# A hybrid encoder step: one table of durations for making and ranking the work, another for ordering each engine's instructions

## The chip, the cores and the metric

The kernel runs on one core of a Trainium2 chip. The core has a matrix engine (TensorE, PE in the profile, with its weight loads shown as PEld), a vector engine (VectorE, DVE), a scalar engine (ScalarE, ACT), a general one (GpSimd, POOL), and a queue that issues most DMAs (SyncE, SP). Each works through its own list of instructions in order, and they meet through semaphores. The metric is the time of one execution on the device in microseconds.

## The reference, cut to what matters

Two layers for a prompt of 2048 tokens and a running stream of 32 further ones, of width 1024, in float32. The first layer is sliding-window attention with ALiBi and sinks, the second a gated DeltaNet; both have a normalization ahead, a SiLU gate and a residual add.

```python
def attn_prompt(h, w_in, sinks, w_out):
    q, k, v, gate = attn_project(h, w_in)
    ...
    o = sink_attention(qb, band(k), band(v), q_pos, k_pos.astype(F32), k_pos >= 0, sinks)
    y = (o * jax.nn.silu(gate)) @ w_out

def gated_delta_chunked(q, k, v, g, beta, s0, chunk):
    ...
    a = m + jnp.eye(chunk, dtype=F32)
    sol = lax.linalg.triangular_solve(a, rhs, left_side=True, lower=True, unit_diagonal=True)
    ...
    def step(s, xs):
        qi, ki, ui, wi, gi, ai = xs
        v_new = ui - jnp.einsum('bhcd,bhde->bhce', wi, s)
        o = jnp.einsum('bhcd,bhde->bhce', qi * jnp.exp(gi)[..., None], s) + jnp.einsum('bhij,bhje->bhie', ai, v_new)
        s = s * jnp.exp(g_last)[..., None, None] + jnp.einsum(
            'bhcd,bhce->bhde', ki * jnp.exp(g_last[..., None] - gi)[..., None], v_new)
        return s, o
```

The large matrix products (both layers' input and output projections) and the many small ones (scores, values, the chain over chunks of 64 tokens) all run on TensorE.

## The kernel before

**How the work is cut.** The prompt's tokens are four slabs of 512 columns (`SLABS`, line 30); the second also carries the 32 sample tokens, and so is cut in two groups of 272. For every slab, a block (class `Block`) is one projection of 128 output rows: eight 128-row steps of the inner dimension, three matmuls each, because every operand is split into a high and a low part of the fast float32 type (`project`). These are the matmuls `pj<-hk,wh` of the profile. Each block's result is taken from one of two banks `pj` by ACT or DVE.

**Sides.** Whatever isn't a projection is written as generators, called sides, which the builder advances between the matmuls of the blocks (`spawn`, `step`). In the attention layer a side (`attend`) computes two scores banks (`ta`), adds the bias and takes the maximum on DVE (`s<-ta,bias`, `mx`), takes the exponential on ACT (`s<-s,mx`), normalizes on DVE (`s<-s,den`), transposes on PE (`tb<-con,s`), copies on ACT (`pt`) and multiplies by the values (`tc<-pt,vt`). In the delta layer, `local_quad` makes the local scores, `inverse` solves the triangular systems on DVE (31 rounds of a product `sub` and a subtraction `tl`, with 32x32 transposes `ml`, `tq`, `trc` around), and `chain_quad` is the chain over chunks: PE `tb<-st,kq`, DVE `r`, PE `tb<-r,btt`, ACT `vn`, PE `tc<-vn,kd`, `tb<-vn,kd` and `tb<-vn,bit`, DVE `st`. Convolution and gates (`conv_block`, `z_block`) run on ACT, DVE and POOL from tiles `cx` and `cy`.

**The first estimate.** Nothing is sent to the engines while the sides run. Every call goes through `Engine.__getattr__` (line 176), which asks `Estimate.note` for a cost and hands an `Op` to `Order.add`. `Estimate` keeps a clock for each engine from two tables, `COST` (a fixed part, one per element, and one for a scalar that is taken from a tile; line 91) and `LAG` (from the end of an instruction on one engine to the start of the next on another; line 82). That clock says when a side may take its next step, hence where in the program its instructions are made, when weight halves are split, and from which matmul on a DMA may be issued. An instruction's rank is its place in this program, less a lead for a few (`EVAC` 400 for taking a bank, `CHAIN` 600 for the chain).

**The order of each engine.** `Order.flush`, called once at the end of each layer, plays all instructions through once more. It keeps a time for each engine; an instruction is ready when what it depends on has ended, plus the lag (`settle`); the engine that is free first takes the lowest rank among its ready instructions, and its clock advances by the instruction's cost. The sequence in which they are taken is the sequence in which each engine has them on the chip. In the kernel before, `flush` uses the costs of `Estimate.note` and its `LAG`. DMAs are played through too: 60 ns on the queue's engine, 1.5 us to start, a transfer time from size, and 0.5 us to land.

Of the kernel before, what the change touches and what calls it, by code (L numbers as in the profile page):

```python
# [12 lines left out]
F32R = mybir.dt.float32r  # L13
AF = mybir.ActivationFunctionType
ALU = mybir.AluOpType
# [7 lines left out]
CH = 64  # L23
# [33 lines left out]
class Block:  # L57
# [3 lines left out]
    def __init__(self, src, run, need=None, ahead=None, pre=None, post=None, ks=range(KT)):  # L61
        self.beside = False
        self.src, self.run, self.need, self.ahead, self.pre, self.post, self.ks = src, run, need, ahead, pre, post, ks
# [13 lines left out]
class Estimate:  # L77
# [4 lines left out]
    LAG = {  # L82
        "tensor": {"tensor": 0, "vector": 200, "scalar": 200, "gpsimd": 200},
        "vector": {"tensor": 256, "vector": 127, "scalar": 130, "gpsimd": 155},
        "scalar": {"tensor": 270, "vector": 145, "scalar": 34, "gpsimd": 160},
        "gpsimd": {"tensor": 200, "vector": 60, "scalar": 75, "gpsimd": 100},
    }
    MEAN = 200
# [11 lines left out]
    def place(self, pool, tag, bufs, name):  # L100
        ring = self.ring.setdefault((id(pool), tag), [])
        self.write[name] = (self.over(pool, tag, bufs), "")
        ring.append(name)
# [67 lines left out]
class Engine:  # L171
# [5 lines left out]
    def __getattr__(self, op):  # L177
        call = getattr(self.engine, op)

        def made(*args, **kw):  # L180
            is_ap = lambda x: isinstance(x, bass.AP)
            outs = [x for x in ([] if "out" in kw else [args[0]]) + [kw.get("out"), kw.get("accum_out")] if is_ap(x)]
            ins = [x for x in list(args[0 if "out" in kw else 1 :]) + [v for k, v in kw.items() if k not in ("out", "accum_out")] if is_ap(x)]
            cost = self.est.note(self.name, op, outs, ins, kw)
            self.order.add(Op(self.name, lambda: call(*args, **kw), cost, op == "dma_start"), ins, outs)  # L185

        return made

# [7 lines left out]
class Op:  # L196


    def __init__(self, engine, call=None, cost=0.0, dma=False):
        self.engine, self.call, self.cost, self.dma = engine, call, cost, dma  # L200
        self.after, self.left, self.ends, self.done, self.rank = [], 0, {}, False, 0
        self.gang = None


class Place:
# [6 lines left out]
class Order:  # L212
# [15 lines left out]
    @contextmanager  # L228
    def together(self):

        self.gang = Op(None)
        self.ops.append(self.gang)
        yield
        self.gang = None

    def place(self, pool, tag, bufs, name):
        ring = self.rings.setdefault((id(pool), tag), [])
# [57 lines left out]
    def settle(self, op):  # L295

        if op.engine:
            lag = lambda by: self.est.LAG.get(by, {}).get(op.engine, self.est.MEAN)
            heapq.heappush(self.wait[op.engine], (max([end + lag(by) for by, end in op.ends.items()] + [0.0]), op.rank, op))
        else:  # L300
            self.finish(op)
# [11 lines left out]
    def flush(self):  # L313

        overs = []
        for p in self.places.values():
            if p.old and p.over is None:
                p.over = Op(None)
                overs.append(p.over)
                for o in p.old.ops:  # L320
                    self.link(o, p.over)
                for o in {id(o): o for o in p.ops}.values():
                    self.link(p.over, o)
                    if o.gang:
                        self.link(p.over, o.gang)
        self.wait = {e: [] for e in self.ENGINES}
        ready = {e: [] for e in self.ENGINES}
        for o in [o for o in overs + self.ops if o.left == 0]:
            self.settle(o)
        while any(self.wait.values()) or any(ready.values()):  # L330
            when = {e: max(self.free[e], 0.0 if ready[e] else self.wait[e][0][0]) for e in self.ENGINES if ready[e] or self.wait[e]}
            e = min(when, key=when.get)
            now = when[e]
            while self.wait[e] and self.wait[e][0][0] <= now:
                _, rank, o = heapq.heappop(self.wait[e])
                heapq.heappush(ready[e], (rank, o))
            _, op = heapq.heappop(ready[e])
            op.call()
            if op.dma:
                self.free[e] = now + 60  # L340
                self.dma = max(now + 1500, self.dma) + op.cost * (self.CLOSE if now < self.START else 1)
                op.ends = {"dma": self.dma + 500}
            else:
                self.free[e] = now + op.cost
                op.ends = {e: self.free[e]}
            op.start = now
            self.finish(op)
        assert all(o.done for o in self.ops)
        self.ops = []
# [1903 lines left out]
```

## Time and profile before

| what | value |
|---|---|
| median of 3 runs | 2374.01 us (2365.21 to 2376.85) |
| the profiled execution's own time | 2376.4 us |
| its span, first to last instruction | 2374.6 us |
| instructions | 44457 |
| POOL's mean for `wh<-wr,wh` 128x512 | 1321 ns |
| DVE's mean for `s<-s,den` 128x256 | 536 ns |

The span is what the profile's rows divide up; the profiled execution's own time is 1.8 us longer. A row that begins with a stretch (`0.00:100.00`) has its length, then each engine's busy time and number of instructions, then the share of its clock that TensorE was granted. A row of a group has busy time, mean duration of one in ns, and the idle time just before them with what ended it. A row of a tile's answer has the least, the median and the most that one took. A releaser in brackets (`<-DVE r`) is what the engine waited for. All instructions of the program carry the line of the recording helper (L185), so they are told apart by their tiles.

### The profile page before, as it was taken

The numbers are of one execution on the slowest core, as the hardware profiler recorded it, in microseconds if no ns is written. First come the engines' busy times: TensorE is split into PE (matmuls) and PEld (weight loads), VectorE is DVE, ScalarE is ACT, GpSimd is POOL, SyncE is SP. The second block draws the span as 40 slices with busy tenths as digits, with TensorE's granted clock in tenths as the row PEclk, the third lists the DMA queues.
The fourth block names the chain that finished last, engine by engine and source line by source line (L and its number), as shares of the span: only waits on it lengthen the run. The fifth ranks groups of instructions, "written<-read, shape, count | busy, mean of one in ns | idle before, by whom it ended". The sixth has DMA issues, their size and how long they took to land.

```text
span 2374.6 us, 44457 instructions
## 1 busy us (share of the span) xinstructions
PE 2252.8 (95%) x14759; PEld 1843.9 (78%) x14759; DVE 1639.6 (69%) x5024; ACT 1262.2 (53%) x3792; POOL 862.9 (36%) x1044
## 2 busy tenths in 40 slices
PE   8998999999999999999999999989999999999997
PEld 5777788797778777777778788877798767777776
DVE  6765465626553445588887768889786888876876
ACT  5555466636553554455566354564644466445533
POOL 4556555665554334222322121331312222122222
PEclk9998999999999999999999999999999999999998
DMA  7556755585434115544423664333456634466442
GB/s 253 175 187 192 255 188 181 174 279 190 147 105 150 62 63 159 193 149 140 143 89 126 200 227 136 128 115 122 147 172 215 200 118 138 134 215 216 155 142 67
DMA packets 222832, 382.75 MB, mean 161 GB/s; under 512 B 29922, under 2 KB 45194, under 8 KB 222602
## 3 DMA queue, kind: packets, MB, share of 16 engines
q1 hardware_dynamic: 220154, 377.75, 49.4%
q8 instruction: 116, 1.90, 0.3%
q10 hardware_dynamic: 2448, 2.16, 0.3%
q14 instruction: 114, 0.93, 0.1%
HBM read 311.63 MB, written 68.19 MB: 160 GB/s over the span
## 4 chain that ended last, share of the span: by engine, by line
PE 56%; DVE 28%; ACT 7%; issue 4%; DMA 3%; POOL 2%; SPq 0%; DVEq 0%; ACTq 0%; POOLq 0%
PE pj L185 39%; PE tb L185 6%; PE ta L185 5%; PE tc L185 4%; DVE cy L185 4%; DVE s L185 3%; DVE sub L185 3%; DVE tl L185 3%; ACT s L185 2%; DVE ml L185 2%; ACT ta L185 1%; DVE xa L185 1%; DVE r L185 1%; DVE md L185 1%; DVE mx L185 1%
## 5 line engine op out<-in xcount | busy, mean ns | idle before, releaser
L185 PE MATMUL pj<-hk,wh 128*128 128x512 f32 (+1 forms) x8184 | 1770.1, 364 | 26.9 <-DVE xr L185 8.6
L185 PEld LDWEIGHTS pj<-hk,wh 128*128 128x128 f32 x8184 | 1326.6, 191 | 237.9 <-issue 14.1
L185 POOL TENSOR_TENSOR wh<-wr,wh 128x512 fp32r<-128x512 f32 x224 | 295.5, 1321 | 328.2 <-ACT wh L185 283.7
L185 DVE SCALAR_TENSOR_TENSOR cy<-cx,cw,cy 128x512 f32<-128x512 f32 x360 | 230.6, 651 | 44.7 <-ACT cy L185 41.1
L185 ACT CAST wh<-wr 128x512 fp32r<-128x512 f32 x224 | 138.1, 618 | 203.6 <-PE pj L185 157.3
L185 ACT ACTIVATE s<-s,mx 128x256 f32<-128x256 f32 (+1 forms) x272 | 132.0, 487 | 30.1 <-DVE mx L185 29.9
L185 ACT ACTIVATE qs<-tb,egq 64x128 f32<-64x128 f32 x264 | 95.7, 362 | 89.7 <-DVE r L185 76.5
L185 DVE TENSOR_TENSOR sub<-ml,tl 128x60 f32<-128x60 f32 (+24 forms) x527 | 125.8, 239 | 10.2
L185 DVE TENSOR_SCALAR s<-s,den 128x256 f32<-128x256 f32 (+1 forms) x272 | 130.9, 530 | 1.2
L185 ACT ACTIVATE cx<-cy 128x512 f32<-128x512 f32 (+1 forms) x96 | 61.1, 636 | 130.9 <-DVE cy L185 101.5
L185 DVE TENSOR_TENSOR tl<-tl,sub 128x60 f32<-128x60 f32 (+24 forms) x527 | 122.3, 232 | 10.1
L185 DVE CUSTOM_DVE_ANT_0 s<-ta,bias 128x256 f32<-128x256 f32 (+1 forms) x272 | 95.7, 405 | 43.5 <-PE ta L185 42.9
L185 POOL TENSOR_TENSOR pr<-pr,ph 128x512 fp32r<-128x512 f32 x82 | 111.8, 1364 | 34.9 <-ACT ph L185 28.8
L185 POOL COPY cx<-hist 128x3 f32<-128x3 f32 x96 | 25.5, 265 | 263.9 <-DVE kq L185 63.6
L185 DVE TENSOR_TENSOR xr<-pj,xr 128x512 f32<-128x512 f32 (+1 forms) x72 | 41.2, 577 | 112.1 <-PE pj L185 70.1
L185 POOL TENSOR_TENSOR so<-so,mhalf 128x4 f32<-128x4 f32 x33 | 36.8, 1115 | 216.9 <-DVE so L185 189.1
L185 DVE SCALAR_TENSOR_TENSOR r<-tb,nbk,vb 64x128 f32<-64x128 f32 x264 | 91.7, 348 | 29.6 <-PE tb L185 25.1
L185 ACT ACTIVATE qs<-o 128x128 f32<-128x128 f32 x132 | 40.7, 308 | 133.8 <-DVE o L185 128.3
L185 ACT COPY cx<-pj 128x512 f32<-128x512 f32 (+2 forms) x149 | 64.1, 445 | 77.5 <-PE pj L185 62.1
L185 PE MATMUL tb<-st,kq 128*128 128x128 f32 x512 | 94.7, 286 | 6.8 <-DVE st L185 5.9
L185 PEld LDWEIGHTS tb<-st,kq 128*128 128x128 f32 x512 | 82.9, 194 | 21.5 <-DVE st L185 13.0
L185 PE MATMUL tb<-con,s 128*128 128x128 f32 (+2 forms) x528 | 77.7, 280 | 18.9 <-DVE s L185 16.0
(242 smaller groups left out, 3558.0 us busy)
## 6 DMA issues: line engine op xcount, KB each, us to landing
wh<-xswwd SPq DMA_DIRECT2D x528, 256.0 KB
wr<-in_wa SPq DMA_DIRECT2D x160, 256.0 KB
wh<-xswwdo SPq DMA_DIRECT2D x112, 256.0 KB
pr<-in_wd SPq DMA_DIRECT2D x66, 256.0 KB
xswwd<-ph SPq DMA_DIRECT2D x66, 256.0 KB
xswwd<-pr SPq DMA_DIRECT2D x66, 256.0 KB
wr<-in_wao SPq DMA_DIRECT2D x64, 256.0 KB
xa<-in_x SPq DMA_DIRECT2D x48, 256.0 KB
```

Of the source, the lines that this page charges most:

```text
L185: self.order.add(Op(self.name, lambda: call(*args, **kw), cost, op == "dma_start"), ins, outs)
```

## The change

`Order` gets tables of its own, `TOOK` and `LAG`, and a method `measure` that writes an instruction's cost anew before it is added; DMAs keep theirs. `Estimate` isn't touched: when sides step, the ranks, the splitting of weights and the DMA's place all still come from the old table. `settle` takes the lag from `Order`, and `flush` adds two things to the cost: 100 ns (`SWITCH`) where a matmul's tile of the array differs from that of the matmul before, and for a DVE operation whose operands all lie in SBUF the time that POOL is still planned to be busy, at most 300 ns (`SHARED`).

```diff
-            self.order.add(Op(self.name, lambda: call(*args, **kw), cost, op == "dma_start"), ins, outs)
+            new = Op(self.name, lambda: call(*args, **kw), cost, op == "dma_start")
+            if not new.dma:
+                self.order.measure(new, op, outs, ins, kw)
+            self.order.add(new, ins, outs)
...
-        self.gang = None
+        self.gang, self.tile, self.shares = None, None, False
...
+    TOOK = {"vector": (150, 1.05, 62), "scalar": (148, 0.845, 100), "gpsimd": (180, 2.17, 0)}
+    LAG = {
+        "tensor": {"tensor": 0, "vector": 205, "scalar": 205, "gpsimd": 230},
+        "vector": {"tensor": 120, "vector": 20, "scalar": 60, "gpsimd": 90},
+        "scalar": {"tensor": 120, "vector": 45, "scalar": 20, "gpsimd": 80},
+        "gpsimd": {"tensor": 120, "vector": 40, "scalar": 40, "gpsimd": 80},
+    }
+    MEAN = 200
+
+    SWITCH, SHARED = 100, 300
+
+    def measure(self, new, op, outs, ins, kw):
+
+        size = lambda x: x.free_size() if callable(x.free_size) else x.free_size
+        out, near = outs[0], all(x.space == bass.MemoryType.SB for x in [*outs, *ins])
+        if new.engine == "tensor":
+            k, m, n = ins[0].shape[0], out.shape[0], size(out)
+            up = lambda n: 32 if n <= 32 else 64 if n <= 64 else 128
+            new.tile = up(k), up(m)
+            if op == "transpose":
+                new.cost = 109.0
+            elif ins[0].dtype == F32R:
+                new.cost = max(107.0, 0.4375 * n + 7) * (0.53 if k == CH else 1)
+            else:
+                new.cost = max(216.0, 4 * n / 2.4 + 4) * {32: 0.2, 64: 0.52}.get(m, 1)
+            return
+        n = max(size(x) for x in [*outs[:1], *ins])
+        fixed, each, more = self.TOOK[new.engine]
+        if op == "transpose":
+            fixed, each = 190, 1.8
+        if new.engine == "gpsimd" and op == "tensor_copy":
+            each = 3.3
+        if new.engine == "vector":
+            if near and op in ("tensor_copy", "tensor_scalar"):
+                each = 0.55
+            new.shares = near
+        if new.engine == "scalar" and ins[0].space == bass.MemoryType.SB:
+            fixed += 50
+        new.cost = fixed + each * n
+        if any(isinstance(kw.get(k), bass.AP) for k in ("scale", "bias", "scalar", "scalar1")):
+            new.cost += more
+        if "accum_out" in kw:
+            new.cost += 188 if new.engine == "scalar" else 82
+        if kw.get("op") == ALU.pow:
+            new.cost += 185 * n + 70
...
-            lag = lambda by: self.est.LAG.get(by, {}).get(op.engine, self.est.MEAN)
+            lag = lambda by: self.LAG.get(by, {}).get(op.engine, self.MEAN)
...
+        tile = None
...
-                self.free[e] = now + op.cost
+                cost = op.cost
+                if e == "tensor":
+                    cost, tile = cost + (self.SWITCH if op.tile != tile else 0), op.tile
+                elif op.shares:
+                    cost += min(self.SHARED, max(0.0, self.free["gpsimd"] - now))
+                self.free[e] = now + cost
```

## The prediction

> **What bounds the kernel now.** I read the page's busy line first, then the granted clock, then the stretches, then PE's own list of waits.
>
> ```profile
> PE 2252.8 (95%) x14759; PEld 1843.9 (78%) x14759; DVE 1639.6 (69%) x5024; ACT 1262.2 (53%) x3792; POOL 862.9 (36%) x1044
> ```
>
> ```profile
> core 0: 2374.6 us, clock 0.978
> ```
>
> ```profile
> core 0: us, PE busy (x) PEld busy (x) DVE busy (x) ACT busy (x) POOL busy (x), PEclk, DMA share, GB/s
> 0.00:100.00 100.00, 86.49 (x483) 63.97 (x485) 70.42 (x163) 59.31 (x143) 50.69 (x47) 1.00 0.70 224
> 100.00:975.00 875.00, 838.68 (x5526) 687.39 (x5523) 465.07 (x1402) 465.68 (x1231) 457.54 (x400) 0.99 0.52 168
> 975.00:2300.00 1325.00, 1268.92 (x8382) 1045.06 (x8380) 1059.57 (x3336) 709.50 (x2331) 339.34 (x578) 0.98 0.49 158
> 2300.00:2375.00 75.00, 58.71 (x377) 47.46 (x377) 44.54 (x125) 27.73 (x91) 15.34 (x20) 0.81 0.18 61
> ```
>
> TensorE is the bound: 95% of the span. The change adds and removes no instruction, so only time in which PE stands still, or runs at a lowered clock, can be won. Idle is length less busy: 13.5 us in the start, **36.3** in the rest of the attention layer (875 - 838.7), **56.1** in the delta layer (1325 - 1268.9), 16.3 in the tail. Start and tail wait for first loads and a last chain; I leave them. The middle holds 92.4 us.
>
> The clock adds to that. A mean of 0.978 loses 0.022 x 2374.6 = 52 us of full-speed time, of which 0.19 x 75 = 14 lie in the tail: **38** in the rest. These losses stand behind PE's stalls:
>
> ```profile
> 178.00:184.00 6.00, 1.59 (x11) 1.13 (x9) 5.05 (x8) 4.01 (x13) 4.34 (x3) 0.90 0.51 142
> 184.00:190.00 6.00, 5.73 (x33) 4.37 (x33) 5.93 (x10) 4.80 (x10) 4.13 (x4) 0.50 0.42 138
> ...
> 2022.00:2029.00 7.00, 2.85 (x14) 2.13 (x15) 6.82 (x16) 3.45 (x13) 6.04 (x9) 1.00 0.28 100
> 2029.00:2032.00 3.00, 3.00 (x12) 1.89 (x11) 2.41 (x12) 1.33 (x5) 0.00 (x0) 0.57 0.00 0
> ```
>
> PE was busy 1.6 of 6 us, and the next 6 us ran at 0.50; it was busy 2.9 of 7 us, and the next 3 ran at 0.57. A long stall is paid twice. [...]
>
> What PE waits for, and where DVE was meanwhile:
>
> ```profile
> PE tb L185 <- DVE s L185: 16.0, 20, 2.5
> PE tb L185 <- DVE r L185: 13.3, 12, 3.7
> PE pj L185 <- DVE xr L185: 8.6, 7, 2.0
> PE tc L185 <- ACT pt L185: 6.9, 5, 4.7
> PE tb L185 <- DVE st L185: 5.9, 9, 1.8
> PE ta L185 <- DVE tq L185: 4.9, 9, 1.8
> PE pj L185 <- DMA wh<-xswwd: 3.0, 5, 0.7
> ```
>
> These are waiter, releaser, us in all, times, longest. And from the timeline around one long stall (start, length, instruction):
>
> ```profile
> 2018.25 2.03 DVE L185 STREAM_TRANSPOSE ml<-md 128x1024 f32<-128x1024 f32 x1
> ...
> 2020.92 1.22 DVE L185 TENSOR_TENSOR ml<-ml,rl 128x1024 f32<-128x1024 f32 x1
> ...
> 2028.01 0.70 DVE L185 SCALAR_TENSOR_TENSOR r<-tb,nbk,vb 64x128 f32<-64x128 f32 x2
> ...
> 2028.77 0.49 PE L185 MATMUL tb<-r,btt 128*128 128x128 f32 x2 [3.70 <-DVE r L185]
> ```
>
> Most named waits are for DVE, and DMA is small. The four timeline rows show the kind: DVE had the inverse's long operations and then its small ones ahead of `r`, while PE's list, fixed at build time, already stood at the matmul that reads `r`. Other matmuls of the projection lay behind it in the list. Such a stall is a misplaced instruction, not a lack of work.
>
> **The change, part by part.** (1) The vector cost becomes 150 + 1.05 n (+62 for a scalar taken from a tile), from 68 + 1.04 n (+60); scalar 148 + 0.845 n, from 52 + 0.83 n. Against the rows (of a tile's answer: least, median, most ns; of the groups: busy us, mean ns):
>
> ```profile
> L185 DVE TENSOR_SCALAR s<-s,den x272: 272/348/1482, 45.8 to 905.4; 128x256 f32<-128x256 f32 x120, 128x128 f32<-128x128 f32 x8, 32x160 f32<-32x160 f32 x8
> ...
> L185 DVE SCALAR_TENSOR_TENSOR r<-tb,nbk,vb x264: 329/350/362, 1041.4 to 2344.0; 64x128 f32<-64x128 f32 x132
> ...
> L185 DVE STREAM_TRANSPOSE ml<-md 128x1024 f32<-128x1024 f32 x17 | 34.7, 2041 | 0.4
> ...
> L185 ACT COPY cx<-pj 128x512 f32<-128x512 f32 x72 | 41.7, 580 | 41.9 <-PE pj L185 34.3 <-DVE kq L185 4.7 <-DVE vf L185 1.5
> ```
>
> For `s` the old table gives 68 + 0.52 x 256 + 60 = 261 ns and the new 353; the median is 348. For `r` 261 and 346; measured 350. For the transpose 1133 and 2033; measured 2041. For the copy 477 and 581; measured 580. So the new durations fit, and the old plan was blind to 82 ns in each of 5024 DVE instructions: 412 us, or 17% of the span. It believed that DVE would come to `s`, `r` and `st` earlier than it can, and set PE's reader there.
>
> (2) PE's own cost: `pj` of 512 columns from 216 to 231 ns, of 272 from 116 to 126.
>
> ```profile
> L185 PE MATMUL pj<-hk,wh 128*128 128x512 f32 x4872 | 1281.5, 408 | 13.0 <-ACT hk L185 4.3 <-DVE hk L185 3.7 <-DVE xr L185 3.2
> L185 PE MATMUL pj<-hk,wh 128*128 128x272 f32 x3312 | 489.4, 298 | 13.9 <-DVE xr L185 5.4 <-ACT cy L185 4.5 <-DMA wh<-xswwd 1.2
> ```
>
> 4872 x 15 + 3312 x 10 = 106 us more in the plan, 4.5% of the span. The old plan ran PE fast too, which hid some of its error about DVE, but 4.5% against 17%. No row times a single one of these, as they overlap; busy over count is 263 and 148 ns, above both tables. SWITCH books 100 ns where PE's tile shape changes and no row isolates it: nothing or 100 in truth, I take it as right; it steers no choice, since the planner still takes the lowest rank that is ready.
>
> (3) The lags shrink: DVE to PE 256 to 120, ACT to PE 270 to 120. In the row above `r` ended at 2028.71 and PE began at 2028.77: 0.06 us, so 120 still has room. With the 82 ns that the duration gains, a lone DVE-to-PE step gets 54 ns shorter in the plan, and four queued `s` 4 x 92 - 136 = 232 ns longer.
>
> (4) Up to 300 ns is added to a DVE operation within SBUF while POOL is planned busy. The rows of the port:
>
> ```profile
> L185 DVE TENSOR_SCALAR mx<-mx x72: 146/170/1290, 43.3 to 901.5; 128x4 f32<-128x4 f32 x64, 32x2 f32<-32x2 f32 x8
> ...
> 198.12 1.19 DVE L185 TENSOR_SCALAR mx<-mx 128x4 f32<-128x4 f32 x1
> ...
> 198.03 1.26 POOL L185 TENSOR_TENSOR wh<-wr,wh 128x512 fp32r<-128x512 f32 x1
> ...
> 199.65 1.55 PE L185 MATMUL tb<-con,s 128*128 128x128 f32 x6 [2.00 <-DVE s L185]
> ```
>
> A four-element operation took 1.19 us instead of 0.17: it began just after POOL's and ended with it (199.31, 199.29), and PE stood 2.00 us. The 300 covers a part of 1.0.
>
> (5) Lists of DVE, ACT, POOL and SP move along with PE's. DMA costs, and the ranks, stay with the old table. SP's issues may come some hundred ns earlier or later against compute; PE's DMA waits are 3.0 us, so I cost that at nothing (bounds: 3 gained; lost, what a later weight load shows, again some 3). The cover is the six `wh` buffers; were it gone, `pj <- DMA` would grow in PE's list.
>
> **The sum.** Attention: much of its wait is the port, of which 300 of some 1000 ns are now planned, so I take a third of 36.3: 12. Delta: the plain durations are the error, and half of 56.1 is 28. Together 40. The clock goes in proportion: 38 x 40 / 92.4 = 16. Every stall that closes brings the next late thing forward (buffers of `cx`, `cy`, two `pj` banks, which DVE and ACT free): I give a third of 56 back, 18. Net 38. The profiled execution took 2376.4 us (span 2374.6, 1.8 around it): 2376.4 - 38 = **2338 us**, 1.5% below the median of 2374.0, which lies 2.4 below the profiled one. Bounds of the unknown share: two thirds of 92.4 with their clock and nothing given back is 62 + 25 = 87, some 2290; nothing at all, 2376.
>
> **The rivals.** *The port decides.* If the 300 ns change nothing, the attention term falls away: 28 + 12 (its clock) = 40, less a third, 26 net: **2350**. The row with 1290 at its most speaks for it, the median of 170 against it. [...]
>
> *The order hardly moves*, or each closed stall is replaced by another: ranks and lists of sides are the old ones, and the planner only departs from rank where something isn't ready. **2374**, within 12. For it: PE has only 5% idle. Against: the `r` stall, with ready matmuls behind it.
>
> *The cushion goes.* The old lags were 136 to 150 ns too long on each step into PE, and so absorbed chance lateness of DVE and ACT. Place: the lone steps of the chains.
>
> ```profile
> L185 PE MATMUL tb<-vn,bit 128*128 128x128 f32 x264 | 65.9, 332 | 0.0
> L185 DVE TENSOR_TENSOR den<-den,es 128x4 f32<-128x4 f32 (+1 forms) x72 | 14.2, 197 | 27.2 <-ACT s L185 20.8 <-ACT es L185 6.0
> ```
>
> Two of the first to a chain step make 132 steps with three entries to PE; 72 attention units have two: 540 entries, each now 54 ns earlier. If all turn into stall, 29 us: **2405** with nothing gained. It decides once the port's uncharged lateness exceeds what the longer durations add; the 0.06 us of real release speaks against it.
>
> **How the numbers follow.** The forecast 0.47 (own range 2295 to 2364), the port 0.15, no change 0.22, the cushion 0.16. Half a per cent is 12 us, about what a measurement here can tell. Faster 0.62, same 0.22, slower 0.16. The range goes from 2295, near the bound of two thirds, to 2388, which takes in all of no change and the milder half of the cushion; some 0.08 lies beyond each end.
>
> **What would show it.** Right: idle before `tb<-con,s`, `tb<-r,btt` and `tb<-st,kq` falls by a third or more, PE's idle in the delta stretch below 35 us, mean clock 0.983 or higher, busy times of DVE and ACT unchanged. The port: the waits for `s` stay near 16 us while those for `r` fall. The cushion: more waits, each short, at the chain's matmuls. I am wrong if PE's idle falls but the span doesn't (busy grows by split matmul runs), or if a transfer shows up in PE's waits.

## The result, and the profile after

The changed kernel took 2439.2 us (median of 4, 2437.7 to 2441.4) against 2372.3 us for the kernel before beside it (median of 4): a ratio of **1.0286** (95% interval 1.0257 to 1.0314), so **2.9% slower**. All ratios below are to the kernel before, timed beside each run.

The profile's page of the changed kernel: span, busy line, and the shares of the chain that ended last.

```profile
span 2439.6 us, 44506 instructions
...
PE 2287.1 (94%) x14759; PEld 1877.0 (77%) x14759; DVE 1642.3 (67%) x5024; ACT 1272.4 (52%) x3792; POOL 866.8 (36%) x1044
...
PE 79%; DVE 12%; ACT 2%; issue 2%; DMA 2%; POOL 2%; SPq 0%; DVEq 0%; ACTq 0%; POOLq 0%
```

The same work on the same engines: DVE 1642 against 1640 us, ACT 1272 against 1262. PE's busy time is 34.3 us longer for the same 14759 matmuls, while the mean granted clock is 0.955 against 0.978; its idle time went from 121.8 to 152.5 us, 30.7 more. Together these are the 65.0 us by which the span grew. The last chain now runs through PE for 79% of its length (56% before). Read alone, that says "PE is the bound, more than before"; the stretches say otherwise. They have the prediction's columns; the last one is longer because the span is:

```profile
0.00:100.00 100.00, 90.72 (x506) 70.28 (x507) 70.54 (x178) 62.52 (x152) 52.09 (x47) 0.98 0.68 225
100.00:975.00 875.00, 849.91 (x5533) 696.98 (x5532) 464.70 (x1396) 469.56 (x1227) 453.19 (x405) 0.98 0.52 170
975.00:2300.00 1325.00, 1234.95 (x8031) 1021.93 (x8030) 1008.36 (x3152) 687.92 (x2242) 331.62 (x555) 0.95 0.47 150
2300.00:2440.00 140.00, 111.55 (x694) 87.78 (x692) 98.74 (x301) 52.45 (x172) 29.90 (x37) 0.83 0.29 92
```

PE's idle time went from 13.5 to 9.3 us in the start and from 36.3 to **25.1** in the attention layer: gains. In the delta stretch it went from 56.1 to **90.1**, and the granted clock there from 0.98 to 0.95. DVE, which was to be relieved of its lateness, is busy for *less* of that stretch: 1008 of 1325 us against 1060. So the attention layer won and the delta layer lost, and there both PE and DVE stand more.

PE's own list of waits for the changed kernel (the columns of the prediction's):

```profile
PE pj L185 <- ACT cy L185: 28.4, 13, 6.2
PE ta L185 <- ACT o L185: 19.6, 10, 6.6
PE ta L185 <- DVE tq L185: 13.7, 8, 7.0
PE ms L185 <- DVE g L185: 10.3, 4, 3.8
PE tb L185 <- DVE s L185: 9.3, 10, 2.5
PE tb L185 <- DVE r L185: 9.0, 12, 1.2
```

The stalls that were to go did shrink: `s` from 16.0 to 9.3 us, `r` from 13.3 to 9.0. In their place stand a few very long ones, 6 to 7 us at worst, for `cy`, `o` and `tq`: things that come late out of DVE and ACT.

The other side of the meeting is the list of waits of ACT and DVE in the delta layer (from 975 us on). Before:

```profile
ACT cx L185 <- PE pj L185: 71.5, 65, 4.7
...
DVE st L185 <- PE tc L185: 56.5, 49, 2.2
DVE r L185 <- PE tb L185: 25.1, 35, 2.5
```

After:

```profile
ACT cx L185 <- PE pj L185: 135.2, 84, 5.1
...
DVE st L185 <- PE tc L185: 82.1, 88, 2.4
DVE r L185 <- PE tb L185: 32.0, 66, 2.1
```

ACT stands nearly twice as long for a projection that PE hasn't ended, and DVE half as long again for `tc`. What that does to the inverse is seen in two tiles' answers (least, median, most ns of one; first to last start). Before:

```profile
L185 DVE STREAM_TRANSPOSE ml<-md x17: 1954/2040/2102, 1010.8 to 2265.5; 128x1024 f32<-128x1024 f32 x17
```

After:

```profile
L185 DVE STREAM_TRANSPOSE ml<-md x17: 1905/2044/2094, 1005.2 to 2336.5; 128x1024 f32<-128x1024 f32 x17
```

Each of the 17 solves begins with one such transpose. The period from solve to solve is (last - first) / 16: 78.4 us before, **83.2** after. Along the solves the whole loss can be laid out: the first solve starts 5.6 us earlier (the attention gain), 16 periods of 4.8 add 76.6, and what follows the last solve's start is 6.0 shorter (109.1 against 103.1): -5.6 + 76.6 - 6.0 = 65.0, the difference of the spans (2439.6 - 2374.6).

Taking DVE's rows from each solve's first `ml` to the end of its `trc`, a solve took 36.2 us before and 43.8 after, as a mean of the 17. Its own operations took 17.2 and 17.7; other DVE work, fitted in between, 16.8 and 19.3; and DVE **stood still for 2.2 and 6.8**. The 4.6 us of added standing is nearly the 4.8 of added period; the other work seems merely to have moved into the solve from the time between two solves, which fell from 41.8 to 38.9. Of the 6.8 us, the largest entry, 1.7, is ahead of `cy<-cx,cw,cy`, which reads what ACT copies out of a projection.

### The profile page after: what moved, and what is told of

It is laid out like the page before. It is cut to its first block, busy times and chain, and to the rows that moved or that the text cites. A ratio compares the mean times of both kernels' runs of the same rounds, so it can differ in the third digit from the quotient of the medians.

```text
span 2439.6 us, 44506 instructions
## 1 busy us (share of the span) xinstructions
PE 2287.1 (94%) x14759; PEld 1877.0 (77%) x14759; DVE 1642.3 (67%) x5024; ACT 1272.4 (52%) x3792; POOL 866.8 (36%) x1044
## 4 chain that ended last, share of the span: by engine, by line
PE 79%; DVE 12%; ACT 2%; issue 2%; DMA 2%; POOL 2%; SPq 0%; DVEq 0%; ACTq 0%; POOLq 0%
PE pj L185 57%; PE tb L185 9%; PE ta L185 8%; PE tc L185 5%; DVE tl L185 2%; DVE sub L185 2%; DVE cy L185 1%; PE ms L185 1%; DVE s L185 1%; DVE hk L185 1%; DVE xa L185 1%; DVE r L185 1%; DMA wh<-xswwd 1%; DMA xa<-xsx 0%; DVE ml L185 0%
## 5 line engine op out<-in xcount | busy, mean ns | idle before, releaser
L185 DVE SCALAR_TENSOR_TENSOR cy<-cx,cw,cy 128x512 f32<-128x512 f32 (+1 forms) x360 | 236.5, 664 | 51.3 <-ACT cy L185 46.5
L185 ACT COPY cx<-pj 128x512 f32<-128x512 f32 (+3 forms) x149 | 65.0, 450 | 164.1 <-PE pj L185 101.4
L185 DVE TENSOR_TENSOR tl<-tl,sub 128x60 f32<-128x60 f32 (+24 forms) x527 | 133.2, 253 | 7.9
L185 DVE TENSOR_SCALAR s<-s,den 128x256 f32<-128x256 f32 (+1 forms) x272 | 119.1, 493 | 2.0
L185 POOL COPY hist<-cx 128x3 f32<-128x3 f32 x96 | 23.0, 240 | 267.2 <-ACT cx L185 245.8
L185 PE MATMUL tb<-st,kq 128*128 128x128 f32 x512 | 105.3, 298 | 3.9 <-DVE st L185 2.1
L185 POOL TENSOR_TENSOR hk<-zs,hk 128x256 fp32r<-128x256 f32 x64 | 49.8, 796 | 155.4 <-ACT hk L185 155.4
L185 POOL COPY cx<-hist 128x3 f32<-128x3 f32 x96 | 37.1, 386 | 184.0 <-DVE kq L185 59.2
L185 DVE SCALAR_TENSOR_TENSOR st<-st,egl,tc 128x128 f32<-128x128 f32 x128 | 44.5, 347 | 84.7 <-PE tc L185 82.1
```

Of the source, the lines that this page charges most:

```text
L185: new = Op(self.name, lambda: call(*args, **kw), cost, op == "dma_start")
```

## The experiments

**Which layer, which half of the tables.** The first runs split the change. e3 uses the new tables in the first `flush` (attention) alone; e1 has the new lags with the old durations, and neither `SWITCH` nor `SHARED`; e2 the new durations with the old lags.

```diff
e3, where an Op is made:
-            if not new.dma:
+            if not new.dma and not self.order.old:
e3, in settle; then, before the delta layer, old = True and SWITCH = 0:
-            lag = lambda by: self.LAG.get(by, {}).get(op.engine, self.MEAN)
+            table = self.est if self.old else self
+            lag = lambda by: table.LAG.get(by, {}).get(op.engine, table.MEAN)
e1:
-            if not new.dma:
+            if False:
-    SWITCH, SHARED = 100, 300
+    SWITCH, SHARED = 0, 0
e2, in settle:
-            lag = lambda by: self.LAG.get(by, {}).get(op.engine, self.MEAN)
+            lag = lambda by: self.est.LAG.get(by, {}).get(op.engine, self.est.MEAN)
```

> The new tables order the first layer, the old ones the second. All theories of a loss in the delta layer: the gain of the first layer (the last value matmul of attention started 8 us earlier after the change) stays and the loss goes: 2358 to 2370. If the attention layer's order hurts the delta layer through what it leaves behind: above 2390.

> Only the lag table is new; durations are the old ones, no SWITCH, no SHARED. Theory A (the loss comes from durations: DVE and ACT are now booked at their real length, PE isn't, so DVE's list waits for PE and the inverse takes longer): near the kernel before, 2360 to 2385, and the mean inverse near its 36 us. Theory B (the loss comes from the shorter lags): most of the loss is here, 2415 to 2440.

> Only the durations (with SWITCH and SHARED) are new; the lags are the old, longer ones. Theory A: most of the loss stays, 2415 to 2450. Theory B: the loss goes, 2350 to 2385.

| run | us | ratio (95%) |
|---|---|---|
| e3, attention alone | 2360.6 | 0.9951 (0.9935 to 0.9967) |
| e1, lags alone | 2504.3 | 1.0551 (1.0488 to 1.0613) |
| e2, durations alone | 2457.5 | 1.0353 (1.0314 to 1.0393) |

e3 keeps the gain and loses the loss: **the loss lies in the order of the delta layer**. Neither expectation for e1 was met, it is slower than both; e2 lies 7 us above theory A's range. Each half by itself is worse in the delta layer than both together: the period of the solves is 84.2 us in e1 and 85.1 in e2, against 83.2. The two halves belong to one another: for a lone small DVE operation whose result PE reads (`r`: 261 or 346 ns, then 256 or 120 of lag), the plan books 517 ns before, 466 after, 381 in e1 and 602 in e2, and both ends are worse than the middle. e1 loses between its solves (52.4 us against 41.8), e2 within them (DVE stands 8.2 us). e1 loses in the attention layer too: its last value matmul `tc<-pt,vt` starts at 939.2 us, against 908.8 before. Why e1 loses in these places was not pursued.

**Is it TensorE's pace?** As a mean, PE's long groups run slower than either table says. From one start to the next of two consecutive `pj` matmuls in the trace after, the median is 234 ns (512 columns) and 125 (272), near the booked 231 and 126; but the mean is 247 and 141, 7 and 12% above (247 and 138 before). A part of this is the lowered clock: without the steps that touch a stretch granted 0.50, the means after are 243 and 136, 5 and 8% above. So in the plan PE runs ahead of the real one, while DVE and ACT now run close to it (`r` booked at 346 ns, median 351 after; `cx<-pj` of 512 columns at 581, mean 586). My theory: DVE's list then has readers of projections and of the chain at places where PE hasn't come yet, DVE stands at them in order, and the inverse behind them stands too. If that is so, booking PE longer should mend it, and shorter should make it worse. In `flush`, with 1.08, 1.16 and 0.92 in e4, e5 and e9:

```diff
-                    cost, tile = cost + (self.SWITCH if op.tile != tile else 0), op.tile
+                    cost, tile = 1.08 * cost + (self.SWITCH if op.tile != tile else 0), op.tile
```

e6 has the 1.08 on the projections' matmuls alone, e7 sets `SWITCH` and `SHARED` to 0:

```diff
e6:
-                new.cost = max(107.0, 0.4375 * n + 7) * (0.53 if k == CH else 1)
+                new.cost = max(107.0, 0.4375 * n + 7) * (0.53 if k == CH else 1.08)
e7:
-    SWITCH, SHARED = 100, 300
+    SWITCH, SHARED = 0, 0
```

> All of the change, and each TensorE cost 8% longer in the plan (512 columns of pj at 249 ns, 272 at 136, where busy over count is 263 and 148). Theory A: the waits of DVE for PE and the loss shrink by half or more: 2370 to 2405. Theory B or another cause: 2425 to 2450.

> The change with all TensorE costs 16% longer in the plan. Theory A (what matters is that the plan's TensorE keeps the pace that it has on the chip; 8% is that pace): past the best, 2380 to 2410. Theory C (the booking of DVE as nearly full pushes the inverse back, and any slower TensorE gives DVE room in the plan): better again, 2345 to 2375, and the mean inverse below the 41.5 us of the 8%.

> The change with all TensorE costs 8% shorter in the plan, about the old table's pace of the projections. Theory A (the plan runs TensorE ahead of the chip, so DVE and ACT stand at instructions that read a projection not yet done): worse than the change, 2465 to 2520, DVE idle inside the inverse's solves above 6.8 us each. If the pace is only one of many random shifts of the order: 2380 to 2455.

> The 8% on the projections' matmuls alone. Both theories: as with 8% on all, 2370 to 2395, since these are 8184 of 14759. If the small matmuls of the chains carry it: 2415 or more.

> The change without SWITCH and SHARED. Theory C: SHARED fills DVE further, so without it somewhat better, 2405 to 2435. Theory A: without SWITCH TensorE is planned faster still, so worse, 2445 to 2475. If the two extras are the cause of the loss: 2360 to 2385.

| PE booked at | us | ratio (95%) | period of the solves | DVE stands in a solve | `cx <- pj` |
|---|---|---|---|---|---|
| 0.92 (e9) | 2519.5 | one run | 87.4 us | 8.7 us | 149.0 us |
| 1.00 (after) | 2439.2 | 1.0286 | 83.2 | 6.8 | 135.2 |
| 1.08 (e4) | 2380.6 | 1.0028 (1.0012 to 1.0045) | 80.3 | 4.8 | 114.7 |
| 1.16 (e5) | 2385.5 | 1.0043 (1.0027 to 1.0060) | 79.9 | 3.3 | 96.7 |
| 1.08, projections only (e6) | 2391.2 | 1.0072 (1.0049 to 1.0095) | 80.8 | 4.6 | 120.0 |
| 1.00, no extras (e7) | 2430.7 | 1.0235 (1.0205 to 1.0264) | 82.6 | 4.5 | 117.6 |

The rows behind two of the table's columns, the tile's answer and the wait. For e9:

```profile
L185 DVE STREAM_TRANSPOSE ml<-md x17: 1898/1991/2092, 1016.7 to 2415.7; 128x1024 f32<-128x1024 f32 x17
```

```profile
ACT cx L185 <- PE pj L185: 149.0, 80, 5.5
```

For e4:

```profile
L185 DVE STREAM_TRANSPOSE ml<-md x17: 1893/2054/2099, 992.2 to 2276.7; 128x1024 f32<-128x1024 f32 x17
```

```profile
ACT cx L185 <- PE pj L185: 114.7, 83, 5.2
```

And for e5:

```profile
L185 DVE STREAM_TRANSPOSE ml<-md x17: 1917/2052/2126, 997.5 to 2275.3; 128x1024 f32<-128x1024 f32 x17
```

```profile
ACT cx L185 <- PE pj L185: 96.7, 74, 4.9
```

One factor on PE's costs in the plan moves the time by 139 us, and period, standing and the wait move with it in order. From 0.92 to 1.08 each 8% is worth some 60 to 80 us; beyond, it is flat. Some 20 of the 139 us lie in the attention layer (the last value matmul starts at 910.6 us in e9, at 890.9 in e4). The attention layer's gain also hides a part of the delta layer's loss: e4's time is near that of the kernel before, but its period of 80.3 us isn't back at 78.4.

Most of the cure comes with the projections alone (e6). e7 missed what my theory gave (2445 to 2475): it is 8.5 us faster than the changed kernel, with intervals that overlap. It takes two extras away at once, of which one made PE longer in the plan and the other DVE, so their effects may offset each other; they weren't run apart. e7 is also out of line in the last two columns: DVE stands as little in its solves as in e6, and ACT waits as little for `pj`, yet its period is 82.6. So neither of these two measures is all of it.

e7 also shows where the attention layer's gain comes from, as it has that gain without `SHARED`. Its row for the stretch and PE's wait for `s`:

```profile
100.00:975.00 875.00, 848.28 (x5540) 697.01 (x5539) 446.42 (x1400) 468.41 (x1229) 452.07 (x405) 0.98 0.53 170
```

```profile
PE tb L185 <- DVE s L185: 6.5, 9, 1.7
```

PE is idle for 26.7 us there, against 25.1 after and 36.3 before, and its last value matmul starts at 900.8 us, against 900.7 after. So the gain doesn't need the 300 ns.

**TensorE's true pace, or the ratio of paces?** e18 leaves PE's booking as the change has it and books every instruction of the other engines, DMAs apart, 8% *short* instead:

```diff
-                cost = op.cost
+                cost = op.cost * (1 if e == "tensor" else 0.92)
```

> The change with TensorE's costs as they are and those of DVE, ACT and POOL 8% shorter than measured. Theory A as a ratio (what counts is TensorE's pace against the others' in the plan, so that making the others wrong cures as well as making TensorE right): near the 8% on TensorE, 2370 to 2402, and DVE's idle time in a solve near 4.8 us. If it is the right booking of TensorE itself that counts: 2425 or more.

2375.0 us, 1.0011 (0.9984 to 1.0038): as good as e4 (PE 1.08). The rows of e18:

```profile
L185 DVE STREAM_TRANSPOSE ml<-md x17: 1911/2046/2101, 993.8 to 2265.5; 128x1024 f32<-128x1024 f32 x17
```

```profile
ACT cx L185 <- PE pj L185: 105.5, 67, 5.4
```

The period is 79.5 us and DVE stands 4.5 us in a solve. So no engine's duration has to be right by itself; **at the new lags, the ratio of the booked durations counts**. The old table booked both engines short, PE by 6% (216 for 231, the median being 234) and DVE's small operations by 25% (`r` 261 for 346, the median being 351), so that against DVE its PE was slow, as in e4, e5 and e18. But it did well only with its own lags: e1 has these same durations with the new lags, and is among the slowest. The ratio of the durations alone isn't the rule; durations and lags make up a plan's pace together.

**Or a fixed lateness?** If PE were only late by a constant, a longer lag would do. e12 books a projection's end 1 us later for the other engines (for every matmul of it, so the release of its weight buffer also comes 1 us later). e16 adds 400 ns to the lag from each other engine into DVE; e17 is e16 with PE at 1.08. e8 gives the inverse's instructions an earlier rank by 600, so that its own operations go first.

```diff
e12:
-                op.ends = {e: self.free[e]}
+                op.ends = {"pj" if op.big else e: self.free[e]}
+        "pj": {"tensor": 0, "vector": 1205, "scalar": 1205, "gpsimd": 1230},
e16, and the same + 400 from scalar and gpsimd:
-        "tensor": {"tensor": 0, "vector": 205, "scalar": 205, "gpsimd": 230},
+        "tensor": {"tensor": 0, "vector": 605, "scalar": 205, "gpsimd": 230},
e8, around each step of the inverse:
-            yield from self.inverse(quads, md, mo)
+            yield from early(self.inverse(quads, md, mo))
+                    self.issue.lead = 600
```

> The change, with TensorE's costs as they are, but the last matmul of each projection is seen by the other engines 1 us later in the plan. Theory A: DVE and ACT reach the readers of a projection later in their lists, DVE's idle time in a solve falls from 6.8 us to below 4.5, and a third of the loss or more goes: 2375 to 2418. If TensorE's pace matters in another way (how many matmuls lie between two steps of a chain): 2425 to 2455.

> The change, and in the plan DVE sees what TensorE, ACT and POOL make 400 ns later, so that its list holds their readers further back, behind more of the inverse's own rounds. Theory E (the solves grow because DVE stands at readers that come too early in its list): idle DVE time in a solve falls from 6.8 us to below 4.5, the solve from 43.8 us to below 41, and a third of the loss or more goes: 2375 to 2418. If standing isn't what matters: 2430 or more, since every chain step is planned 400 ns longer.

> The same with TensorE 8% longer in the plan. Theory E: the two add up in part: 2355 to 2385, the solve near 38 us. Else as the 8% alone or worse, 2380 to 2420.

> The change, and the inverse's DVE and ACT instructions get a lead in rank of 600, as the chain's have. Theory C: the inverse returns to 38 us or less and the loss shrinks by half or more, 2370 to 2405. Theory A: the inverse may shorten, the time stays within 15 us of 2439.

| run | us | ratio (95%) | DVE stands in a solve |
|---|---|---|---|
| e12, projections 1 us late | 2429.6 | 1.0229 (1.0189 to 1.0270) | 6.2 us |
| e16, 400 ns into DVE | 2454.2 | 1.0325 (1.0281 to 1.0369) | 6.3 |
| e17, the same, PE 1.08 | 2385.8 | 1.0032 (1.0012 to 1.0051) | 4.0 |
| e8, inverse first | 2441.9 | 1.0282 (1.0252 to 1.0312) | 6.7 |

None of the three explanations holds. A constant cushion doesn't bring the loss back, whether on the projections (e12: 10 us less than the changed kernel, with intervals that overlap) or on all that DVE reads from other engines (e16 is slower). e17 is no better than 1.08 alone (e4). Rank doesn't help either (e8), which suggests that DVE isn't given the wrong instruction first but stands at one whose input isn't there. All this fits an error that grows along the list, a drift, more than an offset; no run shows the drift itself.

**Or the projections used up too early?** In the trace after, a chain step stands later against the projections than before: 84 more projection matmuls have been issued ahead of it, as a mean. These are PE's cover. Perhaps the loss is that they run out, and the planner should save them. e13 forbids a projection more than 100 ranks beyond the next unfinished chain step, e15 allows 250, e14 is e13 with PE at 1.08.

```diff
+        steps = sorted([o for o in self.ops if o.step], key=lambda o: o.rank, reverse=True)
...
+            while steps and steps[-1].done:
+                steps.pop()
+            if op.cover and steps and op.rank[0] - steps[-1].rank[0] > 100:
+                heapq.heappush(self.wait[e], (now + 100, op.rank, op))
+                continue
```

> The change, and the planner may not take a projection matmul whose rank is more than 100 beyond that of the next unfinished chain step; it waits instead. Theory D (the projections are the cover of the delta layer's chains, the new tables spend it early, and PE runs dry before a slab's end): the matmuls issued ahead of a chain step fall from 84 over the kernel before to about none, the dry spells (165 us in ten) to two or three, and most of the loss goes: 2355 to 2395. Theory E (the inverse's solves are longer because DVE stands at instructions that come too early; early projections only go with it): solves stay above 41 us and the time above 2415.

> The hold at 250 places. Theory D: between the change and the hold at 100: 2375 to 2425. Theory E: 2415 to 2450.

> The same hold with TensorE 8% longer in the plan. Theory D: the two cure the same thing, so little is left to add: 2345 to 2385. Theory E: as with the 8% alone, 2370 to 2392, or worse for the waiting.

e13 took 2465.4 us (1.0382, 1.0352 to 1.0412), e15 2461.7 (1.0366, 1.0336 to 1.0396), e14 2398.4 (1.0100, 1.0064 to 1.0136). In e13 the projections ahead of a chain step are back to before (2 more), and yet it is slower. PE's waits in its delta layer begin with

```profile
PE ta L185 <- DVE tq L185: 62.3, 11, 11.0
```

PE now stands up to 11 us for the end of the inverse. The period is 84.9 us, DVE's standing in a solve still 5.3, and e15 lies above what either theory gave. e4 and e14 say the same from the other side: e4 keeps 57 of the 84 projections ahead and has a period of 80.3 us, e14 has none of them and 81.3. So spent cover isn't needed for the loss, and giving it back doesn't mend it. Whether it is a result of the slow solves wasn't tested.

**The best of both.** e10 and e11 have the old tables in the delta layer. In the attention layer e10 has the change's with PE at 1.08, e11 the new durations with the old lags (in e2 the last value matmul of attention starts at 886.8 us, against 908.8 before and 900.7 after).

```diff
e11, besides e3's:
-            lag = lambda by: self.LAG.get(by, {}).get(op.engine, self.MEAN)
+            lag = lambda by: self.est.LAG.get(by, {}).get(op.engine, self.est.MEAN)
```

> The new tables with TensorE 8% longer in the first layer, the old tables in the second: the first layer's gain (its last value matmul came 18 us earlier with the 8%, 14 without) adds to the old second layer: 2350 to 2362.

> New durations with the old lags in the first layer, the old tables in the second: with these its last value matmul came 22 us earlier, so 2346 to 2360.

e10: 2355.6 us, 0.9919 (0.9894 to 0.9945). e11: **2354.0 us, 0.9907** (0.9875 to 0.9939), some 22 us less than the kernel before (0.0093 x 2372) and 85 less than the changed one, and the fastest of all; e10 can't be told from it.

## Why the prediction was wrong

The forecast was 2338, with slower at 0.16; the time is also above the range. Step by step:

- **(1) Durations.** Right as far as it goes: the new table fits the rows, and the stalls that it was to close (`s`, `r`) shrank by 42 and 32%, near the third that was named; idle before `tb<-st,kq` fell too, from 6.8 to 3.9 us.
- **The attention term**, 12 us: PE's idle there fell by 11.2, and e3 gained 12 us (0.0049 x 2372). Right in sign and size, but the size was luck: the term was put down to the port ("of which 300 of some 1000 ns are now planned"), and e7, which plans none of it, has nearly the same gain (PE idle for 26.7 us there, against 25.1 after). No run shows a port; what the trace before shows is that 11 of the 64 `mx<-mx` of 128x4 took 1.17 to 1.29 us, each ending 24 to 33 ns after a POOL operation that ran beside it, and that the other 53 took at most 0.17 us.
- **The delta term** is the step that failed: "Delta: the plain durations are the error, and half of 56.1 is 28." Idle rose by 34.0 instead. It rests on **(2) PE's own cost**, where I had the fact in hand ("busy over count is 263 and 148 ns, above both tables") and set it aside: PE's part was "4.5% against 17%". I weighed two errors by size, as if mending the larger one alone could only help. They were two errors of one sign. With DVE's and ACT's mended and the lags shortened, the plan runs PE ahead of them, and the dose (0.92, 1.00, 1.08) and e18 show what this ratio is worth in the delta layer: a period of 87.4, 83.2, 80.3 and, in e18, 79.5 us, against 78.4 before.
- I also read **only who PE waits for**. The page's busy line (PE 95%, DVE 69%) made PE the sole bound. From solve to solve the delta layer can also be read as a serial loop through DVE, and rows that might have warned were on the other side: ACT's 71.5 us for `pj`, DVE's 56.5 for `tc`. Both grew. That this loop is what sets the time is my reading; PE is busy for 93% of the delta stretch.
- **The clock term**, 16 gained: its direction followed the idle, its size was off. The mean fell from 0.978 to 0.955; 0.045 x 2439.6 = 110 us of full-speed time lost, against 52. The sum took 0.41 us of clock for each us of idle (38 / 92.4); here 31 us more of idle came with 58 more of lost clock, 1.9 for each.
- **(3) Lags.** The rival *cushion* gave 2405 and had the sign, by a mechanism that isn't this one: it expected many short waits at the chain's matmuls, where PE's wait for `r` fell instead, and neither the old, longer lags (e2) nor fixed cushions (e16, e12) bring the loss back. That lags matter is shown by e1, and in the attention layer the cushion had a point: with the old lags (e2) its last value matmul starts at 886.8 us, with the new ones at 900.7. Step (3) also priced only the lags into PE. The one from a DVE instruction to the next, which each of the inverse's 62 dependent operations pays in the plan, went from 127 to 20 ns. With the 82 ns of added duration such an operation is 25 ns shorter in the plan, not 82 longer; the prediction doesn't name this, and no run changes it alone.
- **(4) `SHARED` and `SWITCH`** are small together: without both, e7 is 8.5 us faster than after. What each does by itself is open.
- **What would show it**: "PE's idle in the delta stretch below 35 us" and "mean clock 0.983 or higher" both failed; "busy times of DVE and ACT unchanged" held.

What stays open. That a *drift* along the list is what stretches a solve is inferred from the dose, the ratio and the failure of every fixed offset; no run isolates the one instruction at which DVE stands, and no run splits the lag from DVE to itself from the others. Why 1.16 closes more of the standing than 1.08 and is no faster, and why e14's hold costs 18 us where e4's kernel without it is even, wasn't settled. No table tried in the delta layer beat the old one; the best period there was e18's 79.5 us, against 78.4.

## What to carry to other kernels

In a planner for engines that run their lists in order, take all engines' durations and the lags as one set: mending one side alone can make the order worse, since the ratio of the booked paces can matter more than whether each duration is right. Before calling an engine the only bound, read the waits of the engines that feed it in the stage in question, and look for a step that repeats there; its period, before and after, shows where time went that the busy shares don't. Adopt such a change stage by stage: here the attention layer's half was worth 0.5 to 0.9% and the delta layer's half cost more than 3%.

## What the runs showed of the hardware

A long stall costs more than I had priced. Stretches around one in the changed kernel (the windows' columns):

```profile
1249.00:1255.00 6.00, 5.27 (x32) 3.95 (x31) 5.36 (x14) 3.60 (x13) 0.00 (x0) 1.00 0.49 175
1255.00:1265.00 10.00, 2.61 (x11) 1.59 (x11) 7.92 (x40) 4.54 (x12) 2.44 (x3) 0.71 0.01 2
1265.00:1274.00 9.00, 2.50 (x10) 2.07 (x11) 7.87 (x34) 4.51 (x13) 2.35 (x5) 0.50 0.04 13
1274.00:1280.00 6.00, 6.00 (x29) 6.00 (x29) 5.52 (x22) 1.35 (x4) 1.84 (x4) 0.53 0.09 29
```

And PE's timeline in it (start, length, instruction, the idle time ahead and its releaser):

```profile
1260.77 1.36 PE L185 MATMUL ta<-con,o 128*128 128x128 f32 x4 [4.72 <-ACT o L185]
1264.80 1.92 PE L185 MATMUL ms<-g,con 128*128 128x36 f32 x8 [2.67 <-DVE g L185]
...
1273.62 1.73 PE L185 MATMUL pj<-hk,wh 128*128 128x272 f32 x6 [6.21 <-ACT cy L185]
```

From 1255 to 1274 us PE was busy for 5.1 of 19 us, with three stalls of 2.7 to 6.2 us, and the clock fell to 0.50. Then PE was full again, and through the next 6 us the grant was still 0.53: 0.50 from 1274 to 1278 us, 0.59 from 1278 to 1280, and 1.00 in the 3 us after. From 1255 to 1280 us the clock cost 0.29 x 10 + 0.50 x 9 + 0.47 x 6 = 10.2 us of full-speed time beside 13.9 us of idle time, 0.73 for each, where the sum took 0.41. DVE was busy for 79 and 87% of the two middle stretches, and PE's three waits there are for ACT and DVE, while the whole span's busy line shows PE at 94%.
